# Feed-forward blocks of a two-layer backbone: seven-product tiles from weight tile 4 instead of 6

## The chip, the cores and the metric

The kernel runs on one core of a Trainium2 chip. The metric is the time of one execution on the device in microseconds (us); lower is better. All times below are of the kernel before the change, from three plain runs and from one execution recorded by the hardware profiler.

## The reference, cut to what matters

Two streams of 256 tokens with 1024 features, the latent tokens (LAT) and the context tokens (CTX), go through two layers. A layer is a half-weighted SwiGLU feed-forward block, a mixer, and a second feed-forward block. Every sub-layer is wrapped in an RMS norm, a shift and scale that depend on a condition vector, and a gate:

```python
def _swiglu_sub(x, mod, j, g_pre, g_post, w_in, w_out):
    h = _modulate_pre(x, g_pre, mod[:, 3 * j], mod[:, 3 * j + 1])
    gate, up = jnp.split(h @ w_in, 2, axis=-1)
    y = (jax.nn.silu(gate) * up) @ w_out
    return _gated_post(x, y, g_post, mod[:, 3 * j + 2], FFN_RES)
...
mod_l = (cond_l @ w_mod[i] + b_mod[i]).reshape(-1, N_MOD, D_MODEL)
```

w_in is 1024 x 5632 and w_out 2816 x 1024. All is fp32. The `mod` vectors (nine of 1024 per layer and stream) come from w_mod, 1024 x 9216 per layer.

## The kernel before, in words

**fp32 out of parts.** A weight tile of 128x2048 arrives in `wraw` (1 MB, queue of SP), ScalarE rounds it to `whi` (L670), VectorE subtracts to get `wlo` (L671). The activations have a high and a low part too, `hhi` and `hlo`, and each product is three matmuls: high by high, low by high, high by low.

**Four feed-forward blocks.** The text calls the second block of layer 0 "block 1" and the first block of layer 1 "block 2". Both handle both streams and both are changed; the two others are not. w_in is cut into 22 weight tiles (NF = 22), each 128 gate and 128 up columns. In block 1 and 2 before the change, `first` does tiles 0 to 2, one stream after the other, while the normed tokens of the second stream are still being made (`pre_t`, L802 to L815). `rest` does tiles 3, 4 and 5 as "plain" tiles: 48 matmuls of 512 columns for both streams. Tiles 6 to 21 go through class `Seven`, the Strassen-Winograd scheme: the tile is a 2x2 block product made from 7 products instead of 8, each 4 steps of 128 by 3 matmuls of 256 columns, so 84 matmuls of 256 columns. For it VectorE makes sums and differences of tokens once per block (`tokens`, L474, L481, and their parts, L490 and L491) and sums of weights once per tile (`load`, L504 to L506, and L520). `convert` makes high and low parts of 128x512 (L525 on ScalarE, L526 on VectorE), and adds to the results (L587, L591, L595) and the SwiGLU products (L596, L598) run on VectorE too.

**The ring.** The parts of the seven products lie in 12 slots (`SLOTS`), four in each of the three `whi`/`wlo` buffers: product n uses slot n mod 12. The same three buffers serve the plain weight tiles ahead of and behind the seven-product stretch, in rotation. The down projection (`out_proj`, 11 chunks of 256 rows of w_out) takes them up again: its chunk 0 takes the next buffer in turn, chunk 1 the one behind it, and each conversion L670 waits for the last product that reads the old contents.

**Down projection and boundary.** `new_parts` splits the activations of a chunk into `ahi` (ScalarE, L1049) and `alo` (VectorE, L1050); TensorE multiplies them with the chunk (`y`, L831, L832 with ahi, L834 with alo). The last chunks are ordered so that a token tile of 128 is done early; its `finish` (L768, L772 on VectorE, L754 on GpSimd, L767, L782 on ScalarE, L788 for the normed `xn`) runs beside the rest. TensorE then transposes `xn` (`tp`, L802) for the next sub-layer.

**The modulation jobs.** The columns of `mod` are made in the background by `mods`: a job loads 512 KB into `mraw` (2 buffers, SP's queue) and VectorE multiplies and sums it, one instruction of 128x1024 (L710) for each stream that needs the column. `mod_rate` says how many jobs a weight tile or a chunk brings; what is still missing is done at once where it is needed (`mods_need`). All streams' jobs of layer 0 come first; the last ones are for LAT alone.

**Order.** TensorE and GpSimd run their instructions in the order of the code. The order of VectorE, ScalarE and the DMA queue is written out when the kernel is built by a scheduler; on the chip each engine then runs its list strictly in that order, and an instruction whose operands are late holds all behind it.

Of the kernel before, what the change touches and what calls it, by code (L numbers as in the profile page):

```python
# [422 lines left out]
NF = FF // 128  # L423
# [178 lines left out]
class Kern:  # L602
# [316 lines left out]
    def ffn(self, layer, which, order, nxt, extra=False):  # L919
# [3 lines left out]
        both = len(order) == 2  # L923
        c0 = 0 if both else 256 * order[0]
        ntok = 256 * len(order)
        with tc.tile_pool(name="act", bufs=1, reuse_waits="tile") as ap:
# [20 lines left out]
                    return [p.rearrange("p (i k n) -> p i k n", i=2, k=8) for p in self.chunk(ahead)]  # L947
                return [p.rearrange("p (k n) -> p k n", k=8) for p in self.chunk(ahead)]

            def first():  # L950
                w = [wv(0), wv(0)]
                for s in range(2):
                    for f in range(3):
                        if f == len(w):
                            w.append(wv(0))

                        split(f, w[f], slice(256 * s, 256 * s + 256), self.h_ready if (s, f) == (0, 2) else None)
                self.mods(3 * self.mod_rate)


            def by_token(f, w, t, a):
# [46 lines left out]
            f = 3  # L1008
            if extra:
                with tc.tile_pool(name="s5v", bufs=1) as vp, ExitStack() as es:  # L1010
                    prep = S5Prep(self, vp, self.dram, self.s5s, self.I["s5b"])
                    self.start(act, wv, swiglu, prep)
                    ep = es.enter_context(tc.tile_pool(name="extra", bufs=1, reuse_waits="tile"))
                    jobs = self.s5_jobs(prep, ep)
                    while f <= max(jobs):
                        rest(f)
                        with tc.issue_after(self.mark), tc.issue_after(self.mark_dma):
                            for job, a in sorted(jobs.get(f, []), key=lambda j: j[0].__name__ in ("pair", "table", "zero")):
                                job(*a)
                        f += 1  # L1020
            elif both and not seven:
                first()
            elif both:
                with tc.tile_pool(name="seven", bufs=1, reuse_waits="tile") as vp:
                    s7 = Seven(self, vp, act)
                    first()
                    for f in range(3, 6):
                        rest(f, min(2, 5 - f))
                        if f < 5:
                            s7.tokens(f - 3)  # L1030
                    self.mod_rate = 0.3 if layer == 0 else 0.4
                    s7.run(range(6, NF))
                    f = NF
            else:
                after = first_single()
                rest(3)
                after()
                f = 4
            with tc.tile_pool(name="fb", bufs=3, reuse_waits="tile") as fb:
                ready = {}  # L1040

                def parts(c):
                    return ready.pop(c) if c in ready else new_parts(c)

                def new_parts(c):
                    hi = fb.tile([128, 2, ntok], F32R, name="ahi")
                    lo = fb.tile([128, 2, ntok], F32R, name="alo")
                    src = act[:, 2 * c:2 * c + 2]
                    nc.scalar.activation(hi, src, AF.Copy)  # L1049
                    nc.vector.tensor_tensor(lo, src, hi.bitcast(F32), op=ALU.subtract)  # L1050
                    return hi, lo

                if f == NF:
                    ready = {c: new_parts(c) for c in range(2)}
                while f < NF:
                    if f == NF - 1:
                        ready = {c: new_parts(c) for c in range(2)}
                    rest(f)
                    f += 1
                finish = self.boundary(layer, j, 0.5, sorted(order), nxt)  # L1060
                self.mod_rate = 3.2 if extra else 4 if layer == 0 else 4.5 if both else 1.75
                self.out_proj(N_FOUT, parts, [t for s in order for t in (2 * s, 2 * s + 1)], finish)

    def s5_jobs(self, pr, pool):
# [458 lines left out]
    def build(self):  # L1523
        nc, I = self.nc, self.I
        self.setup()
        both = (CTX, LAT)
        for i in range(4):
            self.need(list(range(i * CH_FFN, (i + 1) * CH_FFN)))
            if i == 0:
                self.need(list(range(CH_ABIN, CH_QKV)))  # L1530
            if i == 2:
                q = CH_QKV
                self.need([q, q + 4, q + 5, q + 1, q + 2, q + 3, CH_AOUT + 3, CH_AOUT, CH_AOUT + 1, CH_AOUT + 2])
        self.xn, self.h_wait = {}, []
        with self.tc.manual_schedule(engines={mybir.EngineType.PE, mybir.EngineType.Pool}):
            self.mod_rate = 1.2
            self.ffn(0, 0, both, (0, 1, both), extra=True)
            self.mod_rate = 1.75
            self.mixer0((0, 2, both))
            self.mod_rate = 0.9  # L1540
            self.ffn(0, 1, both, (1, 0, both))
            self.mod_rate = 0.9
            self.ffn(1, 0, (LAT, CTX), (1, 1, both))
            self.mixer1((1, 2, (LAT,)))
            self.ffn(1, 1, (LAT,), None)
# [236 lines left out]
```

## Time and profile before

| what | value |
|---|---|
| three runs | 1615.6 to 1621.1 us, median 1617.49 us |
| profiled execution | 1620.71 us |
| its span, first to last instruction | 1618.9 us (1.8 us lie around it) |
| granted TensorE clock, mean | 0.993 of full |
| busy: TensorE matmuls / weight loads | 97% / 86% |
| busy: VectorE / ScalarE / GpSimd | 78% / 44% / 4% |

TensorE is the engine that sets the end nearly everywhere; its busy share is modelled, since matmuls overlap, so what counts is where it waits and at what distance its matmuls start. VectorE is next. The profiled execution is 3.2 us longer than the median of the runs.

### The profile page before, as it was taken

What the parts mean: (1) busy time and instruction counts of PE and PEld (TensorE: products, weight loads), DVE (VectorE), ACT (ScalarE), POOL (GpSimd) and SP (SyncE); (2) the same over time, 40 slices, a digit from 0 to 9 for tenths busy, and PEclk for the clock granted to TensorE, in tenths of its full rate; (3) what the DMA queues carried; (4) which work ended last, traced back from release to release, by engine and by line L of the source; (5) the groups of instructions that cost most, each with busy time, mean ns of one, the idle gap of its engine ahead of it and who ended that gap; (6) DMA issues with size and microseconds to landing.
All of it is one profiled execution on the core that took longest, in us unless ns stands there. A gap on an engine that the chain in (4) does not pass through costs nothing.

```text
span 1618.9 us, 24491 instructions
## 1 busy us (share of the span) xinstructions
PE 1575.4 (97%) x9460; PEld 1393.5 (86%) x9460; DVE 1264.8 (78%) x2498; ACT 712.0 (44%) x1233; POOL 71.7 (4%) x111
## 2 busy tenths in 40 slices
PE   6999999999979999999999999999999999999998
PEld 6888888888879788999988888999988887799986
DVE  6788997877779778899987887899876578686444
ACT  5432323122554453555542353555532266664343
POOL 0000000000110010000000010000000014300000
PEclk9999999999999999999999999999999999999999
DMA  8344665645534323333355533333466432156552
GB/s 344 116 165 162 214 210 200 237 179 206 189 104 166 132 103 108 115 118 131 122 217 207 183 105 118 121 128 121 154 226 245 166 120 105 66 196 247 182 196 103
DMA packets 56548, 264.13 MB, mean 163 GB/s; under 512 B 6432, under 2 KB 10992, under 8 KB 36848
## 3 DMA queue, kind: packets, MB, share of 16 engines
q1 hardware_dynamic: 56432, 262.57, 46.0%
q8 instruction: 74, 1.21, 0.3%
q14 instruction: 42, 0.34, 0.1%
HBM read 254.12 MB, written 8.43 MB: 162 GB/s over the span
## 4 chain that ended last, share of the span: by engine, by line
PE 61%; DVE 5%; ACT 1%; issue 1%; POOL 0%; DMA 0%; DVEq 0%; POOLq 0%; ACTq 0%
PE y L832 7%; PE y L831 7%; PE y L834 7%; PE sa L542 3%; PE sa L543 3%; PE sa L544 3%; PE gu L824 3%; PE gu L825 3%; PE gu L823 3%; PE se L543 2%; PE se L542 2%; PE se L544 2%; DVE wlo L671 1%; PE sf L542 1%; PE sf L543 1%
## 5 line engine op out<-in xcount | busy, mean ns | idle before, releaser
L671 DVE TENSOR_TENSOR wlo<-wraw,whi 128x2048 fp32r<-128x2048 f32 x115 | 263.4, 2291 | 92.9 <-ACT whi L670 92.5
L670 ACT ACTIVATE whi<-wraw 128x2048 fp32r<-128x2048 f32 (+1 forms) x123 | 224.5, 1828 | 203.4 <-PE u L824 76.6
L710 DVE SCALAR_TENSOR_TENSOR junkv<-mraw,cond 128x1024 bf16<-128x1024 f32 x224 | 273.4, 1221 | 19.2 <-DMA mraw<-wmod 17.7
L831 PE MATMUL y<-whi,ahi 128*128 128x512 f32 x616 | 244.5, 397 | 0.0
L832 PE MATMUL y<-wlo,ahi 128*128 128x512 f32 x616 | 243.6, 396 | 0.0
L834 PE MATMUL y<-whi,alo 128*128 128x512 f32 x616 | 198.7, 395 | 0.0
L824 PE MATMUL gu<-hlo,whi 128*128 128x256 f32 x496 | 139.2, 281 | 1.2 <-DVE hlo L815 1.2
L831 PEld LDWEIGHTS y<-whi,ahi 128*128 128x128 f32 x616 | 116.7, 189 | 26.9
L1049 ACT ACTIVATE ahi<-act 128x1024 fp32r<-128x1024 f32 (+1 forms) x44 | 41.5, 950 | 223.6 <-PE y L832 223.6
L834 PEld LDWEIGHTS y<-whi,alo 128*128 128x128 f32 x616 | 116.4, 189 | 27.1
L832 PEld LDWEIGHTS y<-wlo,ahi 128*128 128x128 f32 x616 | 116.6, 189 | 26.8
L823 PE MATMUL gu<-hhi,whi 128*128 128x256 f32 x496 | 138.9, 280 | 0.0
L825 PE MATMUL gu<-hhi,wlo 128*128 128x256 f32 x496 | 138.6, 279 | 0.0
L525 ACT ACTIVATE whi<-wraw 128x512 fp32r<-128x512 f32 x160 | 98.7, 628 | 76.6 <-PE u L824 20.6
L526 DVE TENSOR_TENSOR wlo<-wraw,whi 128x512 fp32r<-128x512 f32 x160 | 107.2, 689 | 3.3 <-ACT whi L525 1.0
L1050 DVE TENSOR_TENSOR alo<-act,ahi 128x1024 fp32r<-128x1024 f32 (+1 forms) x44 | 47.8, 1091 | 74.1 <-ACT ahi L1049 74.1
L824 PEld LDWEIGHTS gu<-hlo,whi 128*128 128x128 f32 x496 | 93.1, 188 | 1.9 <-DVE hlo L815 1.8
L823 PEld LDWEIGHTS gu<-hhi,whi 128*128 128x128 f32 x496 | 93.3, 188 | 0.1
L825 PEld LDWEIGHTS gu<-hhi,wlo 128*128 128x128 f32 x496 | 93.0, 188 | 0.0
L823 PE MATMUL g<-hhi,whi 128*128 128x512 f32 x200 | 79.3, 397 | 0.0
L823 PE MATMUL u<-hhi,whi 128*128 128x512 f32 x200 | 78.5, 392 | 0.0
L824 PE MATMUL u<-hlo,whi 128*128 128x512 f32 x200 | 78.4, 392 | 0.0
(373 smaller groups left out, 3892.0 us busy)
## 6 DMA issues: line engine op xcount, KB each, us to landing
wraw<-wts SPq DMA_DIRECT2D x153, 1024.0 KB, 4.9
mraw<-wmod SPq DMA_DIRECT2D x131, 512.0 KB, 4.2
gg<-gg SPq DMA_DIRECT2D x10, 512.0 KB, 6.0
s5p<-dP SPq DMA_DIRECT2D x8, 384.0 KB, 5.0
act<-wmod SPq DMA_DIRECT2D x5, 512.0 KB, 8.8
act<-wsc SPq DMA_DIRECT2D x5, 512.0 KB, 8.8
dP<-s5cz SPq DMA_DIRECT2D x8, 320.0 KB, 2.3
dP<-s5st SPq DMA_DIRECT2D x8, 320.0 KB, 4.6
```

Source lines behind the costliest of these rows:

```text
L525: K.nc.scalar.activation(hi, src, AF.Copy)
L526: K.nc.vector.tensor_tensor(lo, src, hi.bitcast(F32), op=ALU.subtract)
L542: nc.tensor.matmul(o, w1[:, k], b1[:, k], start=(new and k == 0), stop=False, skip_group_check=not new)
L670: nc.scalar.activation(h, r, AF.Copy)
L671: (nc.gpsimd if pool else nc.vector).tensor_tensor(l, r, h.bitcast(F32), op=ALU.subtract)
L710: nc.vector.scalar_tensor_tensor(self.junk_v, t, 1.0, self.cond[:, s], op0=ALU.mult, op1=ALU.mult, accum_out=self.mod[:, layer, s, idx * 8 ...
L823: nc.tensor.matmul(out, w1, self.hhi[:, k, sl], start=(k == 0), stop=False)
L824: nc.tensor.matmul(out, w1, self.hlo[:, k, sl], start=False, stop=False)
L825: nc.tensor.matmul(out, w2, self.hhi[:, k, sl], start=False, stop=(k == 7))
L831: nc.tensor.matmul(o, ahi, whi[i], start=first, stop=False)
L832: nc.tensor.matmul(o, ahi, wlo[i], start=False, stop=False)
L834: nc.tensor.matmul(o, alo, whi[i], start=False, stop=last)
```

## The change

In blocks 1 and 2, `first` gets the token sums of stream 0 between its two streams, the sums of stream 1 follow, one plain tile (tile 3) remains, and the seven-product stretch covers tiles 4 to 21: 18 tiles instead of 16. The rates of the modulation jobs are set anew: none in `first` and in tile 3 (0 instead of 0.9 per tile), 0.4 per seven-product tile (before 0.3 in layer 0, 0.4 in layer 1), 5.5 per chunk of block 2's down projection (before 4.5; block 1 keeps 4).

```diff
-            def first():
+            def first(between=None):
                 w = [wv(0), wv(0)]
                 for s in range(2):
+                    if s and between:
+                        between()
                     for f in range(3):
...
-                self.mods(3 * self.mod_rate)
+                if not between:
+                    self.mods(3 * self.mod_rate)
...
                     s7 = Seven(self, vp, act)
-                    first()
-                    for f in range(3, 6):
-                        rest(f, min(2, 5 - f))
-                        if f < 5:
-                            s7.tokens(f - 3)
-                    self.mod_rate = 0.3 if layer == 0 else 0.4
-                    s7.run(range(6, NF))
+                    first(lambda: s7.tokens(0))
+                    s7.tokens(1)
+                    rest(3, 0)
+                    self.mod_rate = 0.4
+                    s7.run(range(4, NF))
...
-                self.mod_rate = 3.2 if extra else 4 if layer == 0 else 4.5 if both else 1.75
+                self.mod_rate = 3.2 if extra else 4 if layer == 0 else 5.5 if both else 1.75
...
-            self.mod_rate = 0.9
+            self.mod_rate = 0
             self.ffn(0, 1, both, (1, 0, both))
-            self.mod_rate = 0.9
+            self.mod_rate = 0
             self.ffn(1, 0, (LAT, CTX), (1, 1, both))
```

The change lengthens the file by one line ahead of `new_parts`, so L1049 and L1050 (ahi, alo) read L1050 and L1051 behind it. Three places of VectorE's list differ as follows.

**End of block 1's seven products, start of its down projection.** On VectorE before the change, from the addition of the last tile but one (sa is a TensorE result, wlo the low part of chunk 0 and then of chunk 1, alo that of the activations of chunk 0):

```order
L596 TENSOR_TENSOR act_5011<-gg_7332,act_5011 128x2x128
L671 TENSOR_TENSOR wlo_7574<-wraw_7571,whi_7573 128x2048
L598 TENSOR_TENSOR act_5011<-sa_7317,act_5011 128x2x128
L671 TENSOR_TENSOR wlo_7580<-wraw_7577,whi_7579 128x2048
L587 TENSOR_TENSOR gg_7439<-se_7425,gg_7439 128x256
L591 TENSOR_TENSOR gg_7439<-sf_7426,gg_7439 128x256
L595 TENSOR_TENSOR gg_7439<-sa_7424,gg_7439 128x256
L1050 TENSOR_TENSOR alo_7544<-act_5011,ahi_7543 128x1024
L596 TENSOR_TENSOR act_5011<-gg_7439,act_5011 128x2x128
L598 TENSOR_TENSOR act_5011<-sa_7424,act_5011 128x2x128
L710 SCALAR_TENSOR_TENSOR junkv_82,mod_76<-mraw_7535,cond_73 128x1024
```

and with the change:

```order
L596 TENSOR_TENSOR act_5011<-gg_7442,act_5011 128x2x128
L598 TENSOR_TENSOR act_5011<-sa_7427,act_5011 128x2x128
L671 TENSOR_TENSOR wlo_7684<-wraw_7681,whi_7683 128x2048
L587 TENSOR_TENSOR gg_7549<-se_7535,gg_7549 128x256
L591 TENSOR_TENSOR gg_7549<-sf_7536,gg_7549 128x256
L595 TENSOR_TENSOR gg_7549<-sa_7534,gg_7549 128x256
L671 TENSOR_TENSOR wlo_7690<-wraw_7687,whi_7689 128x2048
L596 TENSOR_TENSOR act_5011<-gg_7549,act_5011 128x2x128
L598 TENSOR_TENSOR act_5011<-sa_7534,act_5011 128x2x128
L710 SCALAR_TENSOR_TENSOR junkv_82,mod_76<-mraw_7645,cond_73 128x1024
L1051 TENSOR_TENSOR alo_7654<-act_5011,ahi_7653 128x1024
```

The low part of chunk 1 (the second L671) stood ahead of the last tile's L587, and alo of chunk 0 right behind its L595. Now that L671, L596, L598 and a modulation instruction L710 stand between L595 and the first alo. In block 2 the same L671, L596 and L598 stand there, without the L710.

**Boundary behind block 1.** VectorE before the change, from the last gating of the second token tile of its first stream (y, L768, and the L710 behind it) to the normed xn that TensorE transposes next:

```order
L710 SCALAR_TENSOR_TENSOR junkv_82,mod_76<-mraw_8071,cond_73 128x1024
L753 SCALAR_TENSOR_TENSOR ssy_8242<-ssy_8242 128x1
L772 SCALAR_TENSOR_TENSOR x_69<-y_7565,ssy_8242,x_69 128x512
L772 SCALAR_TENSOR_TENSOR x_69<-y_7566,ssy_8242,x_69 128x512
L671 TENSOR_TENSOR wlo_8286<-wraw_8283,whi_8285 128x2048
L753 SCALAR_TENSOR_TENSOR ssx_8251<-ssx_8251 128x1
L788 TENSOR_SCALAR xn_8256<-x_69,ssx_8251 128x512 x2
```

and with the change:

```order
L710 SCALAR_TENSOR_TENSOR junkv_82,mod_76<-mraw_8175,cond_73 128x1024
L753 SCALAR_TENSOR_TENSOR ssy_8352<-ssy_8352 128x1
L736 SCALAR_TENSOR_TENSOR ggc_11194<-mod_76,cols_74 128x8
L714 TENSOR_TENSOR mod_76<-mod_76,cols_74 128x8
L710 SCALAR_TENSOR_TENSOR junkv_82,mod_76<-mraw_8181,cond_73 128x1024
L772 SCALAR_TENSOR_TENSOR x_69<-y_7675,ssy_8352,x_69 128x512
L710 SCALAR_TENSOR_TENSOR junkv_82,mod_76<-mraw_8181,cond_73 128x1024
L772 SCALAR_TENSOR_TENSOR x_69<-y_7676,ssy_8352,x_69 128x512
L671 TENSOR_TENSOR wlo_8396<-wraw_8393,whi_8395 128x2048
L753 SCALAR_TENSOR_TENSOR ssx_8361<-ssx_8361 128x1
L736 SCALAR_TENSOR_TENSOR ggc_11194<-mod_76,cols_74 128x8
L788 TENSOR_SCALAR xn_8366<-x_69,ssx_8361 128x512 x2
```

One more modulation job, of two L710, stands there: one ahead of the first L772 and one between the two.

**Boundary behind block 2.** VectorE before the change, from the low part of the down projection's last chunk (the names y, ssy, ssx, xn are as above):

```order
L671 TENSOR_TENSOR wlo_11550<-wraw_11547,whi_11549 128x2048
L714 TENSOR_TENSOR mod_76<-mod_76,cols_74 128x8
L768 TENSOR_TENSOR y_10996<-y_10996,gg_10990 128x512
L768 TENSOR_TENSOR y_10997<-y_10997,gg_10990 128x512
L753 SCALAR_TENSOR_TENSOR ssy_11603<-ssy_11603 128x1
L772 SCALAR_TENSOR_TENSOR x_69<-y_10996,ssy_11603,x_69 128x512
L772 SCALAR_TENSOR_TENSOR x_69<-y_10997,ssy_11603,x_69 128x512
L753 SCALAR_TENSOR_TENSOR ssx_11612<-ssx_11612 128x1
L788 TENSOR_SCALAR xn_11617<-x_69,ssx_11612 128x512 x2
L768 TENSOR_TENSOR y_10998<-y_10998,gg_10990 128x512
L768 TENSOR_TENSOR y_10999<-y_10999,gg_10990 128x512
L753 SCALAR_TENSOR_TENSOR ssy_11656<-ssy_11656 128x1
```

and with the change, in the same place:

```order
L671 TENSOR_TENSOR wlo_11787<-wraw_11784,whi_11786 128x2048
L710 SCALAR_TENSOR_TENSOR junkv_82,mod_76<-mraw_11643,cond_73 128x1024
L710 SCALAR_TENSOR_TENSOR junkv_82,mod_76<-mraw_11646,cond_73 128x1024
L768 TENSOR_TENSOR y_11206<-y_11206,gg_11200 128x512
L714 TENSOR_TENSOR mod_76<-mod_76,cols_74 128x8
L768 TENSOR_TENSOR y_11207<-y_11207,gg_11200 128x512
L753 SCALAR_TENSOR_TENSOR ssy_11840<-ssy_11840 128x1
L772 SCALAR_TENSOR_TENSOR x_69<-y_11206,ssy_11840,x_69 128x512
L772 SCALAR_TENSOR_TENSOR x_69<-y_11207,ssy_11840,x_69 128x512
L710 SCALAR_TENSOR_TENSOR junkv_82,mod_76<-mraw_11650,cond_73 128x1024
L753 SCALAR_TENSOR_TENSOR ssx_11849<-ssx_11849 128x1
L788 TENSOR_SCALAR xn_11854<-x_69,ssx_11849 128x512
```

Three L710, each with its own mraw, stand here among the steps of the first token tile, where none stood. Five more follow: one between its two L788, and four among the steps of the second token tile, the last of them between the two L788 there.

## Rows read from the trace of the kernel before

**Rows 1.** Waits of TensorE: instruction <- releaser: us in total, times, longest.
```profile
PE tp L802 <- DVE xn L788: 5.4, 2, 2.7
...
PE sa L542 <- DVE gg L595: 2.7, 4, 1.0
...
PE s L1416 <- DVE qT L1330: 1.9, 1, 1.9
```

**Rows 2.** TensorE timeline, block 1: start us, us, instruction, [idle before <- releaser].
```profile
652.83 0.39 PE L823 MATMUL g<-hhi,whi 128*128 128x512 f32 x1
...
663.81 0.28 PE L542 MATMUL sa<-hhi,whi 128*128 128x256 f32 x1
...
673.68 0.28 PE L542 MATMUL se<-th,whi 128*128 128x256 f32 x1
...
683.60 0.28 PE L542 MATMUL se<-th,whi 128*128 128x256 f32 x1
```

**Rows 3.** TensorE timeline, start of block 2's seven-product tiles.
```profile
1033.59 0.38 PE L542 MATMUL sa<-hhi,whi 128*128 128x256 f32 x1 [0.35 <-DVE gg L595]
...
1044.17 0.39 PE L542 MATMUL sa<-hhi,whi 128*128 128x256 f32 x1 [0.41 <-DVE gg L595]
```

**Rows 4.** TensorE timeline, first tiles of blocks 1 and 2, second stream.
```profile
615.50 0.39 PE L824 MATMUL gu<-hlo,whi 128*128 128x256 f32 x1 [0.76 <-DVE hlo L815]
...
974.32 0.38 PE L824 MATMUL gu<-hlo,whi 128*128 128x256 f32 x1 [0.17 <-DVE hlo L815]
```

**Rows 5.** ScalarE timeline, end of block 1's seven products.
```profile
816.80 1.92 ACT L670 ACTIVATE whi<-wraw 128x2048 fp32r<-128x2048 f32 x1 [2.33 <-PE sa L543]
```

**Rows 6.** VectorE timeline, the same place.
```profile
818.75 2.29 DVE L671 TENSOR_TENSOR wlo<-wraw,whi 128x2048 fp32r<-128x2048 f32 x1 [2.83 <-ACT whi L670]
...
821.63 0.41 DVE L595 TENSOR_TENSOR gg<-sa,gg 128x256 f32<-128x256 f32 x1
821.96 1.22 DVE L1050 TENSOR_TENSOR alo<-act,ahi 128x1024 fp32r<-128x1024 f32 x1
```

**Rows 7.** TensorE timeline, the same place.
```profile
822.10 0.38 PE L542 MATMUL sa<-hhi,whi 128*128 128x256 f32 x1 [0.96 <-DVE gg L595]
...
824.65 0.63 PE L834 MATMUL y<-whi,alo 128*128 128x512 f32 x2
```

**Rows 8.** VectorE timeline, the same place in block 2.
```profile
1180.95 1.22 DVE L1050 TENSOR_TENSOR alo<-act,ahi 128x1024 fp32r<-128x1024 f32 x1
```

**Rows 9.** TensorE timeline, the same place in block 2.
```profile
1183.65 0.62 PE L834 MATMUL y<-whi,alo 128*128 128x512 f32 x2
```

**Rows 10.** VectorE timeline, boundary behind block 1.
```profile
935.87 1.41 DVE L772 SCALAR_TENSOR_TENSOR x<-y,ssy,x 128x512 f32<-128x512 f32 x2 [0.74 <-POOL ssy L754]
...
940.49 0.88 DVE L788 TENSOR_SCALAR xn<-x,ssx 128x512 f32<-128x512 f32 x2 [0.72 <-POOL ssx L754]
```

**Rows 11.** VectorE timeline, boundary behind block 2.
```profile
1294.40 0.88 DVE L788 TENSOR_SCALAR xn<-x,ssx 128x512 f32<-128x512 f32 x2 [0.72 <-POOL ssx L754]
```

**Rows 12.** TensorE timeline, the transposes behind it.
```profile
1297.05 1.91 PE L802 MATMUL tp<-ident,xn 128*128 128x128 f32 x16
1298.71 0.47 PE L831 MATMUL y<-whi,ahi 128*128 128x512 f32 x1
```

**Rows 13.** The page: costliest instructions (busy, mean ns) and DMA issues (median us to landing).
```profile
L710 DVE SCALAR_TENSOR_TENSOR junkv<-mraw,cond 128x1024 bf16<-128x1024 f32 x224 | 273.4, 1221 | 19.2 <-DMA mraw<-wmod 17.7
...
L526 DVE TENSOR_TENSOR wlo<-wraw,whi 128x512 fp32r<-128x512 f32 x160 | 107.2, 689 | 3.3 <-ACT whi L525 1.0
...
mraw<-wmod SPq DMA_DIRECT2D x131, 512.0 KB, 4.2
```

**Rows 14.** Windows: stretch, length, busy PE, PEld, DVE, ACT, POOL, clock, DMA, GB/s.
```profile
820.00:830.00 10.00, 9.04 (x51) 7.64 (x50) 9.62 (x14) 4.72 (x6) 0.00 (x0) 1.00 0.43 132
...
942.00:946.00 4.00, 4.00 (x17) 3.41 (x15) 3.71 (x13) 3.55 (x8) 0.00 (x0) 0.57 0.47 195
...
1357.30:1363.00 5.70, 5.70 (x20) 4.62 (x21) 4.04 (x11) 2.59 (x6) 2.16 (x4) 0.70 0.51 185
```

## The prediction

> **What bounds the kernel now.** First the page's busy shares and the list of TensorE's waits: TensorE is busy nearly throughout, and in the stretches of the two changed blocks it waits in few places, each for VectorE: 2.7 us in all for L595 in the seven-product stretches, and two waits of 2.7 us for the normed xn, one of them behind block 1 [rows 1]. So a gain here has two sources only, fewer or shorter matmuls and one of those waits. A loss is any spot where VectorE's list, which runs strictly in order, gets later than TensorE's need. Next the timelines of both engines at the seams of the blocks, where those needs are read, and then windows for the clock.
>
> **Plain tile against seven-product tile.** A plain tile runs from one first g matmul to the next tile's start, 652.83 to 663.81: 10.98 us [rows 2]. A seven-product tile is read at the same product of two neighbouring tiles, 673.68 to 683.60: 9.92 us. The change swaps two plain tiles for two seven-product ones in each block, so 4 x 1.06 = **-4.2 us**. VectorE has the work of a tile beside it in either kind (11 instructions of 128x512, five of 128x256), and 0.4 jobs a tile is the rate at which block 2 already runs, so I take the row as it is.
>
> Here a rule speaks against the change. By the Trainium skill, "TensorE: Matmul & The Clock Gate", section "Back-to-back issue gap", a sustained stream of weight loads and matmuls goes at about 81 ns for 128 columns and 131 ns for 512. An estimate from that page of the Trainium skill, a third of the way up for 256 columns (some 98 ns), gives 8.2 us for 84 matmuls and 6.3 us for 48, so that four swaps would cost 7.8 us instead of gaining. The rows above don't agree: 10.98/48 = 0.229 us at 512 columns and 9.92/84 = 0.118 at 256, so columns are paid for and 84 short matmuls are the cheaper tile.
>
> **Two small stalls in block 2 go.** Its first two seven-product tiles wait 0.35 and 0.41 us for L595 [rows 3], with two L710 of the block's entry in front on VectorE. The changed list has no L710 there, since the entry's rate is 0. The first matmul after a wait also takes 0.38 instead of 0.28 us: together **-1.0 us**. Block 1 has no such wait.
>
> **Token sums.** Sums of stream 0 run on VectorE and ScalarE already in the middle of `first` in the kernel before; their places in the list hardly move, and the plain tiles cover them. The new place in the code costs and gains **0**; with that cover gone, VectorE's seven steps of 128x512 for a stream, at 0.69 us as the conversions [rows 13], would be some 4.8 us.
>
> **Start of the seven-product stretch.** It begins where tile 4 began, 22 us earlier, with VectorE having no more to do ahead of it than the time that three first tiles and tile 3 give. One new thing: the first weight sum L504 (128x512, as the conversions of 0.69 us [rows 13]) now stands in the chain that makes the second stream's hhi and hlo. TensorE waits for that chain already, 0.76 us in block 1 and 0.17 in block 2 [rows 4], with VectorE busy without a gap, so a later chain is a later matmul: **+0.6** and **+0.5** (bounds 0 and 0.7 each).
>
> **Start of the down projection, block 1.** The stretch has 18 x 7 = 126 products, not 112. Over 12 slots it ends at another place of the ring: 112 leaves 4 products in the buffer that is begun last, 126 leaves 2 in one that is begun. Chunk 0 and 1 of the down projection then get buffers whose last readers stand 6 and 2 products from the end, before 8 and 4. Two products are 24 x 0.118 = 2.83 us. The low part of chunk 1 needs ScalarE's L670, which started at 816.80 as the products let go of its buffer and took 1.92 [rows 5]: now 819.63 to 821.55. In the order before, L671 (818.75) was followed by L595 at 821.63 and alo at 821.96, and TensorE's first matmul with alo ran at 824.65, where it would have been in any case [rows 6, 7]. In the changed list L595 comes first (TensorE's product before the wait ends 0.96 ahead of 822.10 [rows 7], so at 821.2), then L671 at 821.6, 2.21 to the next start, L596 and L598 at 0.34 each, L710 1.14, and then alo 1.22: done at 826.9. TensorE's first alo matmul, at 824.65 before, runs at 826.95: **+2.3 us** (lower bound 0.5, if the chain starts some 1.8 us earlier; upper 3). TensorE gets there at some 824.2, since its wait ahead of 822.10 is shorter by 0.4, so this is a pause of some 2.7 us.
>
> **The same in block 2.** alo was done at 1182.2 and its matmul ran at 1183.65 [rows 8, 9]. The seams lie 358.99 us apart (821.96 and 1180.95 [rows 6, 8]), so L671 runs 1180.55 to 1182.8, L596, L598, then alo at once: done at 1184.65, so **+1.0** (0 to 1.3).
>
> **Boundary behind block 1.** Fewer jobs at the entry, three, and the job rate of the projection unchanged, leave one job more for the boundary. Two L710 stand ahead of and between the two L772 that started at 935.87 after a wait of 0.74 [rows 10], TensorE waits for the xn behind them already, 2.7 us [rows 1]. Two L710 of 1.22 us [rows 13] less the wait that the first replaces: 1.6; and if mraw is late (its buffer comes free two jobs earlier, by the list some 3.6 us ahead, and it takes 4.2 to land [rows 13]): 0.5 more. I take **+1.6** (1.2 to 2.1).
>
> **Boundary behind block 2.** Eight L710 on the way from the first L768 to the second token tile's L788 (1294.40 to 1295.28) [rows 11], where VectorE now waits for ScalarE and GpSimd between its steps. Walking the new list with each L710 when VectorE is free, the last L788 ends near 1299.8; with each mraw 4.2 us after the L710 two before it, near 1301.2. TensorE needs it about 1.8 us later than it came: its transposes start at 1297.05 and y at 1298.71 [rows 12]. The last four transposes and y come 0.1 and 0.9 after: y at 1300.8 to 1302.1, **+2.2** (1.0, if VectorE's waits take more of the L710, to 3.1). Two jobs that remain are done ahead of the next sub-layer's later tiles, where TensorE has other chunks to run: 0 (to 1.2).
>
> **The clock.** After the 2.7 us wait behind block 1 the granted clock of 942 to 946 is 0.57, that is, the lower of the two levels, 1.2 instead of 2.4 GHz, most of the time; after the wait of 1.9 us [rows 1] it is 0.70 over 1357.3 to 1363; after the 0.96 us at 822.10 [rows 7] it stays 1.00 [rows 14]. (1 - 0.57) x 4 = 1.7 us of TensorE's work, as (1 - 0.70) x 5.7 = 1.7. The new pause at block 1's down projection is as long as the first: **+1.7** (0 to 1.7). Behind block 2 the pause is split by transposes into two of 1 to 1.6 us, in block 2's projection it is some 1.4: between the cases, so I leave them out of the sum and keep 1.7 each for the range. Behind block 1 the clock falls already.
>
> **Sum.** -4.2 - 1.0 + 0 + 0.6 + 0.5 + 2.3 + 1.0 + 1.6 + 2.2 + 1.7 = **+4.7 us**. Against the profiled execution, 1620.71, that is 1625.4; it lies 3.2 us over the median of the runs, so I add the same to 1617.49: **1622.2 us**. About 0.3%, 4.85 us, is what a measurement of this kernel tells from no change.
>
> **Rivals.**
> *VectorE's lateness is hidden; only TensorE's gain is left.* Mechanism: the down projection's chunk 1 is converted as early as before, so alo is ready when wanted, and the L710 of the boundaries go into VectorE's waits (0.74 and 0.72 are seen [rows 10, 11]). For it: VectorE has a fifth of its time free. Against it: the list is fixed, and the buffer's last reader is. It decides if the first alo is done by 824.6. Then -5.2 plus up to 1: 1612.3 to 1613.5, faster.
> *More pauses trip the clock.* The pauses behind block 2 and in its projection each bring 1.7 more, and mraw comes late at both boundaries (+0.5, +0.9): +4.7 + 3.4 + 1.4 = +9.5, 1627, slower. With one of them +6.4, 1623.9. For it: 1.9 us did it. Against it: 0.96 did not, and these are between.
> *The pause at the projection is shorter and the clock stays.* alo is late by half, and no fall: 4.7 - 1.7 - 1.2 = +1.8, 1619.3, no change. For it: one ScalarE step moved by 1 us does that.
> *A seven-product tile costs no less than a plain one where it is put.* Mechanism: a matmul of 256 columns is paced by its weight load, or VectorE is late in tiles 4 and 5 as in block 2's first two. From 10.98/84 = 0.131 us a matmul on the gain is gone: +4.7 + 4.2 = +8.9, 1626.4. Against it: 0.118 in the same block, and even with the waits of [rows 3] a tile is under 10.6. Almost nothing. The Trainium skill's figures above would put it there.
>
> **Chances.** The sum as it stands, within 2 either way, 1620.2 to 1624.2: 0.42, a little over half of it within 0.3% of 1617.49. Shorter pause and no fall, 1617 to 1620.2: 0.22. More falls, above 1624.2: 0.23. Hidden: 0.12, nearly all of it under 1612.6. The dearer tile: 0.01. So faster 0.11; same 0.24 + 0.22 + 0.01 = 0.47; slower 0.18 + 0.23 + 0.01 = 0.42. The range from 1614 to 1627 leaves out the hidden case and the far end of the falls; the likeliest case's own is 1620.2 to 1624.2.
>
> **What would show it.** Right: tiles 4 and 5 at 9.9 us and no wait for L595 at block 2's first two tiles; a wait of TensorE for alo (L834 <- DVE L1051) of 2 to 3 us at the start of block 1's projection with the clock at its lower level behind it, and a shorter one in block 2; the wait for xn behind block 1 at 4 us or more; a new one behind block 2. Wrong: no wait for alo, which would make the ring's phase a mistake of mine; L710 of the boundaries done ahead of the L768; seven-product tiles over 10 us; or a clock that falls at places that I priced at nothing, above all at the hlo waits in `first`, which grow from 0.76 towards 1.4 us.

## The result and the profile after

The changed kernel takes 1626.66 us (median of 11 runs, 1622.2 to 1631.8) against 1617.24 us before (1611.7 to 1621.1): a ratio of 1.0067, 95% interval 1.0054 to 1.0080, some 9 to 13 us slower. (The ratios here are estimated from all runs, with their interval, and can differ a little from the quotient of the two medians.) The forecast was 1622.2 with "no change" as the likeliest outcome. The time lies inside the stated range; the direction was missed.

The profiled execution of the changed kernel took 1622.22 us (span 1620.4 us), its shortest run, and before's 1620.71, one of its longest: read as they are, the two traces differ by 1.5 us. The reason lies ahead of the changed code. Up to the transposes ahead of block 1 the changed execution needed 600.3 us and before's 608.0; over twelve profiled executions, all with the same code there, it is 598.8 to 608.0. So traces are compared from there on, by stretches between fixed instructions: the last transposes ahead of block 1, ggp (L740) at the start of a down projection, the first tp (L802) behind it, and the first matmul of the attention scores (s); the rest ends with TensorE's last matmul.

| stretch, us | before | changed | difference |
|---|---|---|---|
| block 1, to its ggp | 215.7 | 213.5 | -2.1 |
| its projection, to tp | 114.4 | 118.8 | +4.4 |
| boundary and block 2, to its ggp | 244.6 | 244.0 | -0.5 |
| its projection, to tp | 114.4 | 116.1 | +1.7 |
| boundary and mixer, to s | 57.7 | 64.9 | +7.2 |
| the rest | 257.4 | 255.8 | -1.6 |
| sum | 1004.2 | 1013.3 | +9.1 |

The sum agrees with the ratio of the runs. Where TensorE waits in the changed kernel, from the same list as [rows 1]:

```profile
PE tp L802 <- DVE xn L788: 8.7, 6, 4.7
...
PE y L834 <- DVE alo L1051: 3.9, 2, 2.5
PE tp L802 <- DVE v L1351: 3.9, 1, 3.9
PE s L1417 <- DVE qT L1331: 1.6, 1, 1.6
...
PE sa L542 <- DVE gg L595: 1.3, 3, 0.6
```

Two rows are new: a wait for alo, twice, and one of 3.9 us for v, in the attention mixer. The tiles are as forecast: tile 5, plain before, runs from one first product of `se` to the next tile's in 9.91 us, as all later tiles of block 1 do.

```profile
644.51 0.28 PE L542 MATMUL se<-th,whi 128*128 128x256 f32 x1
...
654.42 0.28 PE L542 MATMUL se<-th,whi 128*128 128x256 f32 x1
```

**Start of block 1's projection.** VectorE (start us, us, instruction), to be read against [rows 6]:

```profile
811.82 0.42 DVE L595 TENSOR_TENSOR gg<-sa,gg 128x256 f32<-128x256 f32 x1 [1.00 <-PE sa L544]
812.27 2.29 DVE L671 TENSOR_TENSOR wlo<-wraw,whi 128x2048 fp32r<-128x2048 f32 x1
814.49 0.42 DVE L596 TENSOR_TENSOR act<-gg,act 128x256 f32<-128x256 f32 x1
814.82 0.42 DVE L598 TENSOR_TENSOR act<-sa,act 128x256 f32<-128x256 f32 x1
815.15 1.22 DVE L710 SCALAR_TENSOR_TENSOR junkv<-mraw,cond 128x1024 bf16<-128x1024 f32 x1
...
816.29 1.22 DVE L1051 TENSOR_TENSOR alo<-act,ahi 128x1024 fp32r<-128x1024 f32 x1
```

and TensorE's matmul that waits for it, as in [rows 7]:

```profile
817.57 0.73 PE L834 MATMUL y<-whi,alo 128*128 128x512 f32 x2 [2.55 <-DVE alo L1051]
```

The clock follows, as behind [rows 1]'s wait of 2.7 us (windows as in [rows 14]):

```profile
817.50:821.50 4.00, 3.93 (x11) 3.14 (x12) 4.00 (x5) 0.00 (x0) 0.00 (x0) 0.64 0.71 269
821.50:825.00 3.50, 3.50 (x15) 2.81 (x14) 3.50 (x5) 0.00 (x0) 0.00 (x0) 0.92 0.84 227
...
1179.00:1184.00 5.00, 4.69 (x20) 3.86 (x21) 5.00 (x6) 1.54 (x1) 0.00 (x0) 1.00 0.55 209
1327.30:1331.50 4.20, 4.13 (x16) 3.70 (x17) 4.00 (x15) 2.62 (x8) 0.00 (x0) 0.60 0.00 0
1358.00:1366.00 8.00, 6.44 (x36) 4.96 (x35) 6.79 (x17) 4.29 (x14) 4.50 (x7) 1.00 0.36 132
```

0.36 x 4.0 + 0.08 x 3.5 = 1.7 us of work lost; the third row is the same place in block 2, where the wait was 1.37 us and the clock stays.

**Behind block 2.** TensorE's transposes of xn wait 0.29 and 0.45 us there, little. It is in the mixer, 28 us on, that it stands:

```profile
1327.37 0.87 PE L802 MATMUL tp<-ident,xn 128*128 128x128 f32 x3 [3.89 <-DVE v L1351]
```

The chain of waits, followed back from that instruction (start us, us, what), with the two L710 that were left for the mixer in it (each row `junkv L710 x2` is one L710 and the reading of its sum):

```profile
1298.34 1.14 DVE junkv L710 x2
...
1300.89 1.14 DVE junkv L710 x2
1302.03 2.21 DVE wlo L671
...
1306.45 0.61 DVE y L768
...
1307.29 2.44 POOL ssy L754
1309.75 1.41 DVE x L772 x2
...
1311.24 1.89 ACT whi L670
1313.15 2.29 DVE wlo L671
...
1324.44 0.73 POOL ssh L760
...
1326.89 0.35 DVE v L1351
...
1327.37 0.66 PE tp L802 x2
```

Read it from the top: from 1293 to 1309 us VectorE has no idle time that could take up the two L710. They push L671 and the gating of the next token tile behind them; GpSimd's L754, 0.54 us elsewhere, takes 2.44 here; then VectorE waits 1.72 us for ScalarE's next weight conversion, and the norm of the last token tile comes late with it; GpSimd makes its rotary tables and the norm of k in the order of the code, behind that; and only then is v taken out of the PSUM bank that the third group of transposes writes next. The clock falls behind this wait (0.60 in the fourth window above) and no longer behind the wait for s (1.00 in the fifth, 0.70 before [rows 14]); those 1.7 us cover the -1.6 us of the rest.

### The profile page after: what moved, and what is told of

Same layout as the page of the kernel before. It is cut to its first block, busy times and chain, and to the rows that moved or that the text cites. A ratio compares the mean times of both kernels' runs of the same rounds, so it can differ in the third digit from the quotient of the medians.

```text
span 1620.4 us, 24900 instructions
## 1 busy us (share of the span) xinstructions
PE 1566.0 (97%) x9604; PEld 1389.4 (86%) x9604; DVE 1285.4 (79%) x2554; ACT 725.7 (45%) x1273; POOL 74.7 (5%) x111
## 4 chain that ended last, share of the span: by engine, by line
PE 56%; DVE 9%; ACT 2%; issue 2%; POOL 1%; DMA 1%; POOLq 0%; DVEq 0%; ACTq 0%
PE y L834 6%; PE y L831 6%; PE y L832 6%; PE sa L542 4%; PE sa L544 4%; PE sa L543 4%; PE gu L823 3%; PE gu L824 3%; PE gu L825 3%; PE se L544 2%; PE se L542 2%; PE se L543 2%; DVE wlo L671 2%; DVE junkv L710 2%; PE sf L542 1%
## 5 line engine op out<-in xcount | busy, mean ns | idle before, releaser
L671 DVE TENSOR_TENSOR wlo<-wraw,whi 128x2048 fp32r<-128x2048 f32 x111 | 254.1, 2290 | 71.8 <-ACT whi L670 71.6
L670 ACT ACTIVATE whi<-wraw 128x2048 fp32r<-128x2048 f32 (+1 forms) x119 | 216.7, 1824 | 184.9 <-PE u L824 76.5
L710 DVE SCALAR_TENSOR_TENSOR junkv<-mraw,cond 128x1024 bf16<-128x1024 f32 x224 | 273.4, 1220 | 15.7 <-DMA mraw<-wmod 13.7
L1050 ACT ACTIVATE ahi<-act 128x1024 fp32r<-128x1024 f32 (+1 forms) x44 | 41.3, 949 | 228.6 <-PE y L832 220.3
L525 ACT ACTIVATE whi<-wraw 128x512 fp32r<-128x512 f32 x180 | 111.0, 628 | 72.4 <-DMA wraw<-wts 26.5
L526 DVE TENSOR_TENSOR wlo<-wraw,whi 128x512 fp32r<-128x512 f32 x180 | 119.7, 687 | 5.9 <-ACT whi L525 3.2
L1051 DVE TENSOR_TENSOR alo<-act,ahi 128x1024 fp32r<-128x1024 f32 (+1 forms) x44 | 47.7, 1090 | 79.5 <-ACT ahi L1050 79.5
L542 PE MATMUL sa<-hhi,whi 128*128 128x256 f32 x288 | 80.8, 281 | 1.3 <-DVE gg L595 1.3
L543 PE MATMUL sa<-tl,whi 128*128 128x256 f32 x288 | 81.3, 282 | 0.0
L544 PE MATMUL sa<-th,wlo 128*128 128x256 f32 x288 | 81.1, 281 | 0.0
```

The lines of the kernel that those rows point to most:

```text
L542: nc.tensor.matmul(o, w1[:, k], b1[:, k], start=(new and k == 0), stop=False, skip_group_check=not new)
L543: nc.tensor.matmul(o, w1[:, k], b2[:, k], start=False, stop=False, skip_group_check=not new)
L544: nc.tensor.matmul(o, w2[:, k], b1[:, k], start=False, stop=(k == 3), skip_group_check=not new)
L670: nc.scalar.activation(h, r, AF.Copy)
L671: (nc.gpsimd if pool else nc.vector).tensor_tensor(l, r, h.bitcast(F32), op=ALU.subtract)
L710: nc.vector.scalar_tensor_tensor(self.junk_v, t, 1.0, self.cond[:, s], op0=ALU.mult, op1=ALU.mult, accum_out=self.mod[:, layer, s, idx * 8 ...
```

## The experiments

Ten kernels, each in rounds of five against the kernel before on the same chip. The first four:

**1. The ring alone.**

```diff
-        i = n % self.SLOTS
+        i = (n + 2) % self.SLOTS
```

> The changed kernel with the 126 products begun in slot 2 of the ring, so that the stretch ends on a full buffer of four as before; the modulation jobs stay as in the change. Theory A (the ring's phase makes the low part of chunk 1 and so the first alo of the down projection late, and the pause lowers the clock): TensorE's waits for alo, 2.55 and 1.37 us in the changed kernel, vanish, and 5 to 6 us go; some 1621 us, 1.0025 of before. Theory B (the loss comes from the modulation jobs alone): the time stays at 1626 to 1627, 1.006.

Measured: 1620.76 us against 1616.93, ratio 1.0024 (1.0009 to 1.0038). The waits for alo are gone; VectorE's alo and TensorE's first matmul with it, which waits for nothing:

```profile
815.11 1.22 DVE L1051 TENSOR_TENSOR alo<-act,ahi 128x1024 fp32r<-128x1024 f32 x1
```

```profile
817.80 0.63 PE L834 MATMUL y<-whi,alo 128*128 128x512 f32 x2
```

Both projections take 114.4 us again, and the wait for xn behind block 1 is back at 2.71 us from 4.68, though all jobs are where the change put them. The mixer keeps its 3.9 us, and its stretch takes 66.6 us, more than the 64.9 of the changed kernel: behind the wait for v the granted clock is 0.57 over 1322 to 1330, 3.4 us of work lost instead of 1.7. Theory A holds, and theory B alone falls: there are two losses.

**2. The jobs alone**, as many ahead of each projection as before.

```diff
-                if not between:
-                    self.mods(3 * self.mod_rate)
+                self.mods(3 * self.mod_rate)
...
-                    self.mod_rate = 0.4
+                    self.mod_rate = 0.37 if layer == 0 else 0.46
...
-                self.mod_rate = 3.2 if extra else 4 if layer == 0 else 5.5 if both else 1.75
+                self.mod_rate = 3.2 if extra else 4 if layer == 0 else 4.5 if both else 1.75
...
-            self.mod_rate = 0
+            self.mod_rate = 0.9
```

(the last one ahead of both blocks).

> The changed kernel with as many modulation jobs done ahead of each block's down projection as before (0.9 a tile at the block's entry, 0.37 and 0.46 a seven-product tile, 4.5 in block 2's projection); the ring stays as in the change. No L710 is left in the boundary behind block 2 nor ahead of the attention mixer. Theory B (those ten L710 delay the chain of norms there; the 3.9 us wait in the mixer is their child): that wait falls to the 0.2 us of before, about 5 us go, 1 comes back at block 2's first two tiles: some 1622 to 1623 us, 1.003. Theory A alone: no change, 1626. Theory C (the mixer's wait comes from another bank of PSUM that the tiles' count hands it): the 3.9 us stay, with the L710 gone.

Measured: 1625.01 us, 1.0052 (1.0036 to 1.0067), a smaller gain than expected; by the runs alone it can't be told from the changed kernel (1.0054 to 1.0080). In the trace the mixer's wait is gone, and its stretch is at 57.7 us:

```profile
PE tp L802 <- DVE xn L788: 7.3, 2, 4.6
...
PE y L834 <- DVE alo L1050: 5.1, 2, 2.5
...
PE sa L542 <- DVE gg L595: 2.2, 5, 0.5
```

Theory C falls, since the count of tiles is the same. But block 2's projection now waits 2.54 us for alo, not 1.37, since an L710 stands ahead of the first alo on VectorE here as in block 1; the granted clock behind it is 0.78 over 1189.4 to 1197 where the changed kernel's stays at 1.00, and the projection takes 118.8 us: what the mixer gave, the longer pause took in part.

**3. Both together.**

> Both edits together. If A and B each hold and add up, the waits for alo and the mixer's wait are gone and the gain of the four tiles is seen: some 1615 to 1617 us, 0.999 of before, with the boundary behind block 1 still longer. If either is wrong: 1620 or more.

Measured: 1622.58 us, 1.0036 (1.0022 to 1.0050): a miss. Both losses are gone (projections 114.4, mixer 58.1 us), but block 1 takes 217.3 us and the stretch to block 2's ggp 248.7: TensorE waits near the start of the seven-product stretch, 1.38 us in block 1 and 3.60 in block 2, where the granted clock is 0.80 over 1025.6 to 1034 behind it.

```profile
PE sa L542 <- DVE gg L595: 7.5, 5, 3.6
```

VectorE is late there because it waited itself, for a weight tile. On SP's queue the tile's load stands behind three loads of modulation jobs (VectorE, then the queue):

```profile
1011.96 0.69 DVE L504 TENSOR_TENSOR xn<-wraw 128x512 f32<-128x512 f32 x1 [2.92 <-DMA wraw<-wts]
```

```profile
993.07 10.45 SPq L708 DMA_DIRECT2D mraw<-wmod  x3
1004.39 4.03 SPq L498 DMA_DIRECT2D wraw<-wts  x2
```

In block 1 the same wait is 2.67 us. Neither edit does it alone. Experiment 2 has the same jobs and differs from this kernel by the ring's start only; there the tile's load stands ahead of the third job's, and the two stretches take 213.9 and 245.4 us. Experiment 1, with the same ring and no jobs at the entry, takes 214.8 and 242.5. So the scheduler's order of that queue is the cause found in the trace; a kernel with that order alone put right was not run.

**4. The rates alone, on the kernel before.**

```diff
-                self.mods(3 * self.mod_rate)
+                if not seven:
+                    self.mods(3 * self.mod_rate)
...
-                    self.mod_rate = 0.3 if layer == 0 else 0.4
+                    self.mod_rate = 0.45
...
-                self.mod_rate = 3.2 if extra else 4 if layer == 0 else 4.5 if both else 1.75
+                self.mod_rate = 3.2 if extra else 4 if layer == 0 else 5.5 if both else 1.75
...
-            self.mod_rate = 0.9
+            self.mod_rate = 0
```

(again the last one ahead of both blocks).

> The kernel before with only the modulation jobs moved as the change moves them (none at the blocks' entry, 0.45 a seven-product tile over 16 tiles, 5.5 in block 2's projection), tiles 4 and 5 plain, 112 products. Theory B: +4 to +6 us, some 1622, 1.003, with TensorE waiting in the mixer for v and behind block 2 for xn. Theory A or C alone: no change within 1 us apart from 1 us won at block 2's first two tiles.

Measured: 1622.42 us, 1.0038 (1.0022 to 1.0054), with 16 tiles and the old ring. The same wait stands in the mixer, and none for alo:

```profile
PE tp L802 <- DVE xn L788: 7.2, 6, 2.7
...
PE tp L802 <- DVE v L1351: 3.9, 1, 3.9
PE sa L542 <- DVE gg L595: 1.9, 2, 1.0
```

So moving the jobs costs some 6 us by itself (by stretches +5.9: +7.7 from the boundary behind block 2 to s, -1.2 in the rest, -0.7 from the boundary behind block 1 to block 2's ggp); the two further seven-product tiles have no part in that.

**5 to 7. Which L710, and the token sums.** On the kernel of experiment 1, block 2's tiles at 0.55 jobs:

```diff
-                    self.mod_rate = 0.4
+                    self.mod_rate = 0.4 if layer == 0 else 0.55
```

> The kernel of the run with the ring begun in slot 2, and block 2's seven-product tiles at 0.55 jobs instead of 0.4, so that no job is left for the attention mixer: the two L710 inside its first chain of hhi and hlo are gone, while seven L710 still stand in the boundary ahead of it. Theory B1 (the two L710 in the mixer's chain delay it): TensorE's wait of 3.9 us for v falls to near nothing, some 5 us less than with the ring alone, 1616. Theory B2 (the boundary's own L710 are the delay, handed on to the mixer): the wait stays above 3 us, no gain, 1621.

Measured: 1618.48 us against 1616.69, 1.0006 (0.9988 to 1.0024). The wait for v is 0.56 us and the stretch to s 59.0 us, from 66.6 in experiment 1, with seven L710 still in the boundary; VectorE is late at more tiles of block 2 instead (waits for L595 5.0 us in all, 3.2 in experiment 1):

```profile
1308.38 0.54 POOL L754 TENSOR_TENSOR ssy<-ssy,mh 128x1 f32<-128x1 f32 x1 [12.46 <-DVE ssy L753]
```

```profile
1308.95 1.41 DVE L772 SCALAR_TENSOR_TENSOR x<-y,ssy,x 128x512 f32<-128x512 f32 x2 [0.74 <-POOL ssy L754]
1310.28 2.28 DVE L671 TENSOR_TENSOR wlo<-wraw,whi 128x2048 fp32r<-128x2048 f32 x1
```

```profile
1324.94 1.06 PE L802 MATMUL tp<-ident,xn 128*128 128x128 f32 x8 [0.56 <-DVE v L1351]
```

Theory B1 holds in the trace: the two L710 inside the mixer's chain are the loss, and the boundary's own cost 1.3 us (59.0 against 57.7). The intervals of experiments 1 and 5 overlap, so the runs' times alone don't decide it; by stretches the trace is 4.4 us shorter than that of experiment 1.

What the two L710 do is more than their own 2.3 us. With them gone, the scheduler's list has L671 behind L772, as above, and as in the kernel before; with them, in the changed kernel and in experiments 1 and 4, L671 stands ahead of L772 (1307.03 and 1309.75 in the changed kernel), and L754 takes 2.43 us. How much of the loss is this order and how much the L710 themselves was not tried apart.

With 0.66 and block 2's projection at 4.5:

> The ring begun in slot 2, block 2's seven-product tiles at 0.66 jobs and its projection at 4.5: one L710 is left behind the first L772 of the boundary, none in the mixer. Both B1 and B2: the stretch from the transposes behind block 2 to the scores is as short as before (57.7 us), 1615 to 1616 us, 0.999 of before. If the higher rate makes VectorE late in the seven-product tiles, the waits for L595 there grow and eat it: 1618.

Measured: 1616.33 us, 0.9989 (0.9976 to 1.0002). The stretch to s is 57.6 us, and block 2 has four waits of 0.4 us for L595, so both halves of the expectation came true in part. With the jobs in the tiles, six of block 2's tiles take 10.2 to 10.6 us instead of 9.9, 3.4 us in all: much of what the four tiles were to win goes there.

The kernel before with only the token sums moved:

```diff
-                    first()
+                    first(lambda: s7.tokens(0))
+                    s7.tokens(1)
                     for f in range(3, 6):
                         rest(f, min(2, 5 - f))
-                        if f < 5:
-                            s7.tokens(f - 3)
```

> The kernel before with only the token sums written where the change writes them (stream 0's between the two streams of the first tiles, stream 1's behind them), tiles 3 to 5 plain, rates as before. By the prediction's step this moves nothing: 1617 us, within 0.1% of before. A rival: VectorE's list changes in the second stream's chain and TensorE's wait for hlo there, 0.76 us, grows by 0.6 in each block: 1618.4.

Measured: 1616.81 us, 1.0008 (0.9993 to 1.0023): nothing to be told from no change, and the wait for hlo is 0.74 us. The rival falls.

**8 to 10. Adding up, and a better version.** The changed kernel with its own ring and the rates of experiment 6:

> The changed kernel with its ring as it is, and only block 2's rates set so that no job is left for the mixer and two L710 for the boundary (0.66 a seven-product tile, 4.5 in the projection). If the two causes add up, the loss at the ring stays (waits for alo 2.5 and 1.4 us, lower clock) and the mixer's goes: 5 to 6 us below the changed kernel, 1621 us, 1.0025 of before, as the ring alone did. If they don't add up (the mixer's wait came about through the earlier pauses): 1618 or less, or 1625 and more.

Measured: 1623.31 us against 1616.95, 1.0043 (1.0028 to 1.0059), between the two outcomes. The mixer's loss is gone (57.6 us) and the ring's is larger than in the changed kernel: 119.3 and 117.7 us for the projections, 5.1 us of waits for alo. The causes are separate. Block 2's pause for alo is 2.51 us here, with an L710 ahead of alo as in experiment 2, against 1.37 in the changed kernel (the clock stays at 1.00 behind it here), and the stretch ahead of it is 248.1 us, with seven waits for L595, five of them of 0.4 us: the rates that free the mixer cost something of their own.

The ring of experiment 1 with 0.5 in block 1, 0.55 in block 2 and 4.75 in its projection:

> The ring begun in slot 2 with the jobs spread over both blocks: 0.5 a seven-product tile in block 1, 0.55 in block 2, 4.75 in block 2's projection; none in the mixer, two L710 more in the boundary. The waits of 0.4 us for L595 that 0.66 jobs a tile brought in block 2 should be fewer: 1615 us, 0.998 to 0.999 of before. If 0.5 is too much for block 1, where each job is two L710, waits for L595 show there: 1617.

Measured: 1615.99 us, 0.9996 (0.9981 to 1.0012). Waits for L595 are 4.5 us in all, so the spreading brought nothing.

17 tiles:

```diff
-        i = n % self.SLOTS
+        i = (n + 1) % self.SLOTS
...
-                    rest(3, 0)
-                    self.mod_rate = 0.4
-                    s7.run(range(4, NF))
+                    rest(3, 1)
+                    rest(4, 0)
+                    self.mod_rate = 0.42 if layer == 0 else 0.7
+                    s7.run(range(5, NF))
```

(and block 2's projection at 4.5).

> Seven products from tile 5: 17 tiles, 119 products, the ring begun in slot 1 so that it ends on a full buffer; rates 0.42 and 0.7, block 2's projection at 4.5. Half of the four tiles' gain: two swaps of 1.06 us and block 2's first waits gone, no loss at the ring or the mixer: 1615 to 1616 us, 0.999, within 1 us of the kernel with 18 such tiles and the same repairs. If a seven-product tile in the place of tile 4 cost anything by itself, this one would be clearly below that.

Measured: 1614.92 us, 0.9989 (0.9976 to 1.0003). It is as good as experiment 6; both intervals include no change, and the gain expected was some 2 us.

## Why the prediction was wrong

By its own steps, with the difference of the stretches:

- **Tiles, -4.2.** Right: 9.91 us a tile, block 1 shorter by 2.1.
- **Block 2's first waits, -1.0.** Right for the two tiles, 9.9 us each from 10.52 and 10.57; but two later tiles take 10.24 and 10.32, so some 0.5 is left. (The fall of the waits for L595 from 2.7 us [rows 1] to 1.3 has another 0.9 in it that is no gain: the wait at the end of each stretch is shorter, and the one for alo follows it.)
- **Token sums, 0.** Right (experiment 7).
- **L504 in the second stream's chain, +1.1.** Too high: the wait for hlo is 0.62 us in block 1 and 0.23 in block 2, against 0.76 and 0.17 [rows 4]. The bound of 0 was the value.
- **First alo in block 1, +2.3 and 1.7 for the clock.** Right in mechanism and size: alo behind L671, L596, L598 and L710 as foretold, a wait of 2.55 us for 2.7, a clock at 0.64, +4.4 for the stretch. Experiment 1 removes all of it.
- **The same in block 2, +1.0.** A little low: +1.7.
- **Boundary behind block 1, +1.6.** The wait grew by 2.0, with two L710 where they were foretold, but the reason given, one job more, does not hold. The wait is 4.6 to 4.7 us in the three kernels with 18 tiles and the ring as in the change (the changed kernel, experiments 2 and 8), though experiment 2 has as many jobs ahead of the projection as before; it is 2.7 us wherever the ring's start was shifted (experiments 1, 3, 5, 6, 9 and 10). So these 2 us belong to the ring's loss. How a projection that begins late brings the L710 there was read from the list, not tried apart.
- **Boundary behind block 2, +2.2, and the two jobs left, 0.** This is the step that failed: "Two jobs that remain are done ahead of the next sub-layer's later tiles, where TensorE has other chunks to run: 0 (to 1.2)." The stretch cost 7.2 us, of which the clock gave back 1.6 further on: +5.7 against 2.2. The boundary itself was priced too high: its waits for xn are 0.74 us, and experiment 5, with seven L710 left in it, takes 1.3 us more in this stretch and 1.3 less in the rest than the kernel before. The two L710 were priced far too low: without them, in experiment 5, the two stretches together are 5.7 us shorter than in the changed kernel. I looked at the first chunks that TensorE runs behind them, which indeed did not wait, and stopped there. They stand on VectorE, which has no idle time behind them until 1309 us, and the scheduler's list around them is another one; what follows in that list, and on GpSimd behind it, came late by their 2.3 us and more, and the bill is presented 25 us on, at the PSUM bank of v.

By stretches, forecast and measured: block 1 -1.5 and -2.1, its projection +4.0 and +4.4, boundary and block 2 -1.0 and -0.5, its projection +1.0 and +1.7, mixer and rest +2.2 and +5.7. The last makes up 3.5 of the 4.4 us between +4.7 and +9.1. That "no change" came out as likeliest is owed to that one zero. That the time still lies inside the range is luck: the range reached up to 1627 for falls of the clock behind block 2's boundary and in its projection, and neither came.

What stays open: the shifted ring costs block 1 some 1.2 us (214.8 against 213.5 in experiment 1). Of these, 0.45 are the wait for L595 at the stretch's end, 0.96 us there, as before, and 0.52 in the changed kernel; the other 0.8 are two tiles of 10.28 and 10.35 us instead of 9.91, and why these two are longer was not followed up.

## What to carry to other kernels

A background job that is left over need not cost where it is done, but where the chain behind it is first waited for: follow VectorE's list from the job to its next idle gap, and each engine that it feeds, before a zero is written down. A count of items that shares a ring of buffers with the next stage fixes which buffer comes free last; choose the starting slot so that the last group is a full one, and look at the order of the loads at the start again (experiment 3). And where executions differ by more than a change is worth in code that the change does not touch, compare traces by stretches, not by their spans.

## What the hardware showed that was not expected

**Short pauses and the clock.** Behind pauses of TensorE of 1.37 us (block 2's projection in the changed kernel), 1.46 and 1.56 us (the mixer) the granted clock stayed at 1.00. Behind 1.87 us (the mixer in experiments 3 and 7), 1.90, 2.55, 2.70 and 3.89 us it fell to its lower level, 1.2 GHz, and some 1.7 us of work were lost. The length of the pause alone does not decide it, though. The wait for xn behind block 1 is 2.70 to 2.72 us in nine of the traces: the clock falls behind it in the kernel before and in experiments 3, 4 and 7, and stays at 1.00 in experiments 1, 5, 6, 9 and 10. In experiment 1 (as in [rows 14], where the kernel before has 0.57):

```profile
934.00:942.00 8.00, 7.80 (x42) 6.63 (x43) 7.09 (x21) 6.73 (x12) 0.00 (x0) 1.00 0.32 124
...
1322.00:1330.00 8.00, 6.82 (x22) 5.76 (x23) 6.84 (x24) 3.92 (x11) 1.06 (x2) 0.57 0.00 0
```

The second row is the place behind its wait of 3.90 us for v: 0.43 x 8 = 3.4 us of work lost, twice what the changed kernel lost behind the same wait. So 1.7 us for each such pause can't be counted on; why the clock falls behind one pause of 2.7 us and not behind another, no run here shows. At the wait for s the traces agree: behind 1.87 to 1.90 us it fell in all three executions that have it, behind 1.56 or 1.57 in none of nine.

**GpSimd held up by VectorE.** L754, on 128x1, takes 0.54 us at seven of the eight places around the mixer, and 2.43 at the one where VectorE runs L671 of 128x2048 beside it, ending some 0.4 us after that:

```profile
1307.29 2.43 POOL L754 TENSOR_TENSOR ssy<-ssy,mh 128x1 f32<-128x1 f32 x1 [14.50 <-DVE ssy L753]
```

```profile
1307.03 2.29 DVE L671 TENSOR_TENSOR wlo<-wraw,whi 128x2048 fp32r<-128x2048 f32 x1
```

In experiments 1 and 4, where L671 stands beside it too, it takes 2.43 us again; in experiment 5, where L671 comes behind L772, it takes 0.54. The Trainium skill, "SBUF — State Buffer", section "Who interferes with whom", states that a VectorE instruction with two inputs in SBUF, as L671 has, contends with a GpSimd instruction that reads SBUF. The trace agrees; 1.9 us of the late chain are that.

**The start.** Of the 7.7 us by which the two profiled executions differ ahead of block 1, 6.0 have come about by 55 us. In both, matmuls of 512 columns start 0.43 us apart at first and 0.23 us apart later; in the execution before the pace changes at 47.95 us, in the changed one ahead of 38.9:

```profile
47.52 0.60 PE L1678 MATMUL g<-hlo,whi 128*128 128x512 f32 x1
47.95 0.40 PE L1679 MATMUL g<-hhi,wlo 128*128 128x512 f32 x1
48.19 0.39 PE L1677 MATMUL u<-hhi,whi 128*128 128x512 f32 x1
```

```profile
35.85 0.63 PE L1679 MATMUL u<-hlo,whi 128*128 128x512 f32 x1
36.28 0.63 PE L1680 MATMUL u<-hhi,wlo 128*128 128x512 f32 x1
...
38.87 0.40 PE L1679 MATMUL g<-hlo,whi 128*128 128x512 f32 x1
39.10 0.40 PE L1680 MATMUL g<-hhi,wlo 128*128 128x512 f32 x1
```

That is the clock. In the changed execution the trace has it at the lower level until 37.0 us (windows, columns as in [rows 14]):

```profile
28.00:36.70 8.70, 8.70 (x29) 7.55 (x30) 8.58 (x19) 5.81 (x10) 0.00 (x0) 0.50 0.94 371
...
38.00:42.00 4.00, 4.00 (x22) 3.38 (x22) 3.92 (x11) 2.37 (x5) 0.00 (x0) 1.00 1.02 407
```

In the execution before, the trace's list of clock levels begins only at 48.0 us, at 1.00, and a window ahead of that reads 1.00 for want of an entry; the pace of the matmuls is that of the lower level. Eleven us more at half the clock are 5.5 us, and a fall at 420 us, which the changed execution does not have, costs another 1.7: 7.2 of the 7.7 us. In all twelve executions the clock comes to its full level at some moment from 32.2 to 48.0 us and keeps it until 418 us or later, and the time to block 1 goes with that moment: 598.8 us where it is 32.2 (experiment 4), 602.0 at 39.0 (1), 605.0 at 45.1 (10), 608.0 at 48.0 (before). So most of the scatter ahead of block 1 is the clock of the first 50 us; what sets that moment, no run here shows.
